# Gate columns of the modulation as running sums on VectorE, with weights loaded one k tile at a time

## The chip, the cores and the metric

The kernel runs on one core of a Trainium2 chip. The metric is the device time of one execution in microseconds (us), from several runs; less is better. Five engines work beside each other, each with a queue of its own that it works off in order: PE (TensorE: matmuls, and the loads of their weights as PEld), DVE (VectorE), ACT (ScalarE), POOL (GpSimd) and SP (SyncE, which here only issues transfers). Semaphores tie the queues together.

## The reference

One step of a network of one layer, on 128 context tokens and 256 latent tokens (384 in all), model width 4096. What matters here:

```python
mod = jax.nn.silu(c) @ w_ada + b_ada            # c_ctx for the context tokens
shift, scale, gate = jnp.split(mod, 3, axis=-1)  # 3 x 4096 columns
u = _rms_norm(h, norm_w) * (1.0 + scale) + shift
out, states = _mixer(u, ...)   # u @ w_in, 8 retention and 16 gated delta heads, both ways, @ w_out
h = h + gate * out
y = _rms_norm(h, final_norm_w)
```

`w_ada` is 4096 x 12288, `w_in` 4096 x 16448, `w_out` 4096 x 4096, all fp32. The modulation is wanted for two vectors only, that of the context and that of the latents. Shift and scale are needed before the input projection, the gate only after the output projection.

## The kernel before

**Projections.** A weight is used in k tiles of 128 rows (`NK` = 32 of them). A *piece* of a `Gemm` is one k tile of a group of 512 columns: its weights (128x512 fp32) land in a buffer `raw`, ScalarE rounds them into `wh` (L209), VectorE puts the rest into `wl` (L210), and PE multiplies both with the high and low part of the activations, `uh` and `ul`: 12 matmuls of 128x384 for a group of kind T (L258 to L260), 9 of 128x512 for kind N (L264 to L266). `wh` and `wl` are rings of `RING` = 5 tiles. Below, a weight tile is one such piece.

**Loads.** SP issues them in `load_piece` (L199): one call brings two k tiles, as two transfers of 256 KB, one for each run of 256 columns. The buffers `raw` are three; the gate pieces use them too.

**Stages.** Until about 770 us the shift and scale columns are computed (class `Ada`, tile `ada`) beside the first part of the input projection, whose partial sums are kept or spilled. Then the rest of the input projection follows, group after group: for each of eight p two groups of kind T and two of kind N. Beside it run the mixers: `gdn` (two gated delta heads, with a triangular solve on VectorE, L854 and L856) and `ret` (a retention head). The mixers are Python generators in `bg_list`. Each `yield` gives a time in ns, `slot(ns)` counts the matmul time that PE's queue has been given since, and when it is used up the next step is emitted (`bg_step`). `pace` stretches or shortens the steps, so that a head is done when its results are due; what is late at a due point is emitted at once (`bg_drain`). From about 2780 us the output projection runs, eight groups of 32 weight tiles. Its first group also fetches the mixers' results (`mix_load`, tile `mixl`, two buffers; `mix_put` splits them into `uh` and `ul`).

**Gate columns.** Class `Ada`, tile `adg`: for 512 columns 16 pieces. A piece loads four k tiles of 256 columns (512 KB) and issues four matmuls with the two vectors as the stationary side (`cst`, padded to 32 columns), each in another quarter of the array's columns (L322), so that the four row groups of the result hold four partial sums. `gate_done` copies them to SBUF on ScalarE, adds the four with a matmul by `sel` (L1184), adds the bias on VectorE and stores the rows in `d_gate`, from where the output projection fetches them, spread over the partitions. The 128 gate pieces are laid between the weight tiles of the N groups.

**Order.** `run_pieces` walks through the list of pieces. Loads and splits (`prepare`) are emitted ahead of the matmuls (`compute`), up to `room` pieces of a kind. So each engine's queue follows this list.

Of the kernel before, what the change touches and what calls it, by code (L numbers as in the profile page):

```python
# [7 lines left out]
F32 = mybir.dt.float32  # L8
F32R = mybir.dt.float32r
AF = mybir.ActivationFunctionType  # L10
ALU = mybir.AluOpType
# [4 lines left out]
D = 4096  # L16
NK = 32
T = 384
# [23 lines left out]
ADA_RING = 6  # L42
# [10 lines left out]
GATE = 1500  # L53
FMAX = 1.0
# [11 lines left out]
def hybrid_step(ctx: ExitStack, tc: tile.TileContext, x_prompt, x_sample, state_ret_fwd, state_ret_bwd,  # L66
# [35 lines left out]
    half_c = const.tile([128, 2, 12], F32, name="half_c")  # L102
    mid_ctx = ExitStack()
# [5 lines left out]
    cst = mid.tile([128, 2 * NK + 32], F32, name="cst")  # L109
    sel = mid.tile([128, 2], F32, name="sel")  # L110
# [81 lines left out]
    def load_piece(src, chunks, k0, nk, ring=None):  # L192
        shape = [128, nk, len(chunks), chunks[0][1]]
        if ring:
            raw = ring(shape)
        else:
            raw = wpool.tile(shape, F32, tag="raw", name="raw", bufs=3)
        for i, (c0, cn) in enumerate(chunks):
            SP.dma_start(out=raw[:, :, i, :],  # L199
                         in_=src[k0 * 128:(k0 + nk) * 128, c0:c0 + cn].rearrange("(k p) n -> p k n", p=128))  # L200
        return raw
# [11 lines left out]
    class Gemm:  # L213
# [6 lines left out]
        def __init__(self, kind, src, chunks, ks, done, pre=None, rows=None):  # L220
            self.kind, self.src, self.chunks, self.done, self.pre = kind, src, chunks, done, pre
            self.ks = ks
            self.rows = rows or (lambda k: k)
            self.ps = self.ps_alloc = self.raw = None
            self.batch, self.lend = 2, None
            self.hold = []
            self.pieces = [(self, i) for i in range(len(ks))]

        def prepare(self, i):
            if i % 2 == 0:  # L230
                self.raw = load_piece(self.src, self.chunks, self.rows(self.ks[i]), min(2, len(self.ks) - i))
            return split_tile(self.raw[:, i % 2], [128, 2, 256], self.lend and self.lend(i))

        def compute(self, i, hl):
# [16 lines left out]
            for n, ps in enumerate(self.ps):  # L251
                for m, (h, lo) in self.hold:
                    k = self.ks[m]
                    st, sp = m == 0, m == end
                    if self.kind == "T":
                        wh = h[:, n // 2, (n % 2) * 128:(n % 2) * 128 + 128]
                        wl = lo[:, n // 2, (n % 2) * 128:(n % 2) * 128 + 128]
                        PE.matmul(ps, wh, high(k), start=st, stop=False)  # L258
                        PE.matmul(ps, wh, low(k), start=False, stop=False)  # L259
                        PE.matmul(ps, wl, high(k), start=False, stop=sp)  # L260
                        slot(3 * 160)
                    else:
                        a, b = high(k)[:, n * 128:n * 128 + 128], low(k)[:, n * 128:n * 128 + 128]
                        PE.matmul(ps, a, h, start=st, stop=False)  # L264
                        PE.matmul(ps, a, lo, start=False, stop=False)  # L265
                        PE.matmul(ps, b, h, start=False, stop=sp)  # L266
                        slot(3 * 213)
                if i == end:
                    self.done(n, ps)
# [4 lines left out]
    class Gates:  # L274
# [9 lines left out]
        def prepare(self, i):  # L284
            raw = load_piece(w_in, [(16384, 64)], i, 8)
            return split_tile(raw[:, :, 0], [128, 8, 64])
# [14 lines left out]
    class Ada:  # L301
# [6 lines left out]
        def __init__(self, c0, width, ps_alloc, done, ring=None):  # L308
            self.c0, self.width, self.ps_alloc, self.done, self.ring = c0, width, ps_alloc, done, ring
            self.ps = None  # L310
            self.pieces = [(self, i) for i in range(0, width // 256 * NK, 4)]

        def prepare(self, i):
            return load_piece(w_ada, [(self.c0 + 256 * (i // NK), 256)], i % NK, 4, self.ring)

        def compute(self, i, raw):
            if self.ps is None:
                self.ps = self.ps_alloc()
            cs = slice(256 * (i // NK), 256 * (i // NK) + 256)
            for q in range(4):  # L320
                k = i % NK + q
                PE.matmul(self.ps[32 * q:32 * q + 32, cs], cst[:, 2 * k:2 * k + 32], raw[:, q, 0],  # L322
                          start=(k < 4), stop=(k >= NK - 4), tile_position=(0, 32 * q))
            slot(450)
            if i + 4 == self.width // 256 * NK:
                self.done(self.ps)
            return 1

# [18 lines left out]
    def run_pieces(pieces):  # L347
# [7 lines left out]
        out = {"do": 0, "ada": 0, "w": 0}  # L355
        room = {"do": len(pieces), "ada": ADA_RING - 1, "w": RING - 1}
        kind = lambda o: "do" if isinstance(o, Do) else ("ada" if isinstance(o, Ada) and o.ring else "w")
# [20 lines left out]
    V.tensor_copy(sel, con[:, C_SEL:C_SEL + 2])  # L378
# [795 lines left out]
    def gate_done(i):  # L1174
        def done(ps):
            sb = [mx.tile([128, T], F32, tag="gsb", name="gsb", bufs=2)[:, 0:256] for _ in range(2)]
            for j in range(2):
                A.copy(sb[j], ps[:, 256 * j:256 * j + 256])
            urgent.append(fin(ps, sb))

        def fin(ps, sb):
            yield GATE
            for j in range(2):
                PE.matmul(ps[0:2, 256 * j:256 * j + 256], sel, sb[j], start=True, stop=True)  # L1184
            yield
            c0 = 512 * i
            for j in range(2):
                G.dma_start(out=sb[j][0:2], in_=b_ada[0, 2 * D + c0 + 256 * j:2 * D + c0 + 256 * j + 256].partition_broadcast(2))
            yield 2000
            for j in range(2):  # L1190
                V.tensor_tensor(sb[j][0:2], ps[0:2, 256 * j:256 * j + 256], sb[j][0:2], op=ALU.add)
                G.dma_start(out=d_gate[:, c0 + 256 * j:c0 + 256 * j + 256], in_=sb[j][0:2])
        return done

# [19 lines left out]
    ada_q = []  # L1214
    for i in range(8):
        ada_q += Ada(2 * D + 512 * i, 512, lambda: ps_main.tile([128, 512], F32, tag="mm3", name="adg"), gate_done(i)).pieces
    for g, (kind, chunks) in enumerate(groups):
# [5 lines left out]
        if kind == "T":  # L1223
            pieces += gm.pieces
        else:
            n, rest = len(gm.pieces), 0
            if g % 2:
                rest = min(8, n // 2)
                cnt = len(ada_q) - 16 * (7 - g // 4)
            else:  # L1230
                cnt = min(16, max(0, 16 * n // (n + NK - reached.get(g + 1, 0) - 8)))
            pieces += gm.pieces[:LEAD] + interleave(gm.pieces[LEAD:n - rest], ada_q[:cnt]) + gm.pieces[n - rest:]
            ada_q = ada_q[cnt:]
    assert not ada_q
# [19 lines left out]
    def open_out():  # L1254
        bg_drain()
# [85 lines left out]
    run_pieces(pieces)  # L1341
# [52 lines left out]
```

## Time and profile before

| | |
|---|---|
| median of 3 runs | 3356.45 us (3355.21 to 3360.35) |
| the profiled execution | 3351.84 us, its span 3350.1 us |
| granted clock of TensorE | 0.991 |
| PE busy | 3254.2 us (97% of the span) |
| VectorE busy | 1845.3 us (55%) |
| ScalarE busy | 1201.5 us (36%) |
| moved by DMA | 626.14 MB, 187 GB/s on average |

PE's busy time counts matmuls from their start to a modelled end, so busy is not the same as at full speed. A row of a group has the line, engine, operation, what it writes and reads, how many, then the busy time and the mean duration of one in ns, and the idle time before them. The chain is the sequence of work, followed back from the last instruction, that set the end; it names at each moment one engine or transfer. In the rows of the transfers the last number is the median time from issue to landing.

### The profile page before, as it was taken

To read this page: it belongs to the slowest core of one execution; us is meant where nothing else is said; L and a number is where in the kernel's file an instruction comes from. 1 tells how busy PE (TensorE), PEld (TensorE's weight loads), DVE (VectorE), ACT (ScalarE), POOL (GpSimd) and SP (SyncE) were. 2 spreads that over 40 slices of the span, in tenths; PEclk is the share of its full clock that TensorE was granted. 3 is DMA by queue.
4 is the path that set the end of the run, shared out by engine and by line. 5 is a ranking of instruction groups with operands and counts; after the bars stand their busy time and mean duration, and the time that the engine had idled before them with its cause. 6 is when DMAs were issued, how large, how long until landed. Compare 5 with 4: busy or idle time off the path is not lost.

```text
span 3350.1 us, 51853 instructions
## 1 busy us (share of the span) xinstructions
PE 3254.2 (97%) x19312; PEld 2694.5 (80%) x19312; DVE 1845.3 (55%) x3811; ACT 1201.5 (36%) x2588; POOL 292.7 (9%) x463
## 2 busy tenths in 40 slices
PE   5999999999999999999999999999999999999998
PEld 2878888877799789689689689779779877788886
DVE  3664444337747646755756746746744855444444
ACT  3322222224244344244244244245244334333333
POOL 0000000001011011001011011011000002100000
PEclk7999999999999999999999999999999999999999
DMA  9989998965535545545644545554544555645445
GB/s 327 308 289 303 324 303 282 303 189 171 160 92 151 166 138 167 167 142 150 186 145 143 172 138 152 173 156 141 172 152 142 159 153 186 188 145 169 146 150 176
DMA packets 594237, 626.14 MB, mean 187 GB/s; under 512 B 38978, under 2 KB 577042, under 8 KB 593984
## 3 DMA queue, kind: packets, MB, share of 16 engines
q1 hardware_dynamic: 570096, 551.04, 52.0%
q0 software_dynamic: 23888, 71.79, 7.2%
q8 instruction: 151, 2.47, 0.3%
q14 instruction: 102, 0.84, 0.1%
HBM read 590.37 MB, written 32.33 MB: 186 GB/s over the span
## 4 chain that ended last, share of the span: by engine, by line
PE 81%; DVE 7%; DMA 6%; issue 3%; ACT 1%; SPq 1%; POOL 0%; ACTq 0%; POOLq 0%; DVEq 0%
PE mm L258 11%; PE mm L260 10%; PE mm L259 10%; PE mm L264 10%; PE mm L265 9%; PE mm L266 9%; PE ada L322 3%; DMA raw<-in_w_in_dram 3%; DVE tmp L854 3%; PE o L265 2%; PE o L266 2%; PE o L264 2%; DVE wl L210 2%; DMA mixl<-d_mix 2%; PE adg L322 1%
## 5 line engine op out<-in xcount | busy, mean ns | idle before, releaser
L210 DVE TENSOR_TENSOR wl<-raw,wh 128x512 fp32r<-128x512 f32 x1274 | 855.3, 686 | 947.4 <-ACT wh L209 931.6
L209 ACT CAST wh<-raw 128x512 fp32r<-128x512 f32 x1274 | 757.5, 620 | 1388.5 <-DMA raw<-in_w_in_dram 567.7
L264 PE MATMUL mm<-wh,uh 128*128 128x512 f32 x1920 | 782.4, 408 | 12.3 <-ACT rawt L564 5.9
L265 PE MATMUL mm<-wl,uh 128*128 128x512 f32 x1920 | 756.5, 394 | 18.0 <-DVE wl L210 17.4
L266 PE MATMUL mm<-wh,ul 128*128 128x512 f32 x1920 | 751.6, 391 | 0.0
L258 PE MATMUL mm<-uh,wh 128*128 128x384 f32 x2048 | 716.8, 350 | 4.1 <-DVE ul L555 2.7
L260 PE MATMUL mm<-uh,wl 128*128 128x384 f32 x2048 | 685.8, 335 | 0.0
L259 PE MATMUL mm<-ul,wh 128*128 128x384 f32 x2048 | 685.1, 335 | 0.0
L264 PEld LDWEIGHTS mm<-wh,uh 128*128 128x128 f32 x1920 | 361.3, 188 | 144.9 <-issue 44.2
L265 PEld LDWEIGHTS mm<-wl,uh 128*128 128x128 f32 x1920 | 361.7, 188 | 103.5 <-DVE wl L210 36.4
L258 PEld LDWEIGHTS mm<-uh,wh 128*128 128x128 f32 x2048 | 384.7, 188 | 48.7 <-issue 25.0
L266 PEld LDWEIGHTS mm<-wh,ul 128*128 128x128 f32 x1920 | 361.1, 188 | 76.7 <-DVE ul L1249 0.3
L259 PEld LDWEIGHTS mm<-ul,wh 128*128 128x128 f32 x2048 | 385.1, 188 | 3.9 <-issue 2.9
L260 PEld LDWEIGHTS mm<-uh,wl 128*128 128x128 f32 x2048 | 384.4, 188 | 0.0
L854 DVE TENSOR_TENSOR tmp<-M 48x4 f32<-48x4 f32 (+14 forms) x240 | 188.3, 784 | 3.4
L322 PE MATMUL ada<-adar,cst 128*32 128x256 f32 x2048 | 146.8, 403 | 23.4 <-DMA adar<-in_w_ada_dram 23.4
L645 DVE SCALAR_TENSOR_TENSOR acc<-rawt,cw,acc 128x126 f32<-128x126 f32 (+3 forms) x384 | 133.5, 410 | 11.9 <-ACT acc L640 11.9
L265 PE MATMUL o<-wl,uh 128*128 128x512 f32 x354 | 138.1, 390 | 0.9 <-DVE wl L210 0.9
L264 PE MATMUL o<-wh,uh 128*128 128x512 f32 x354 | 137.9, 389 | 1.0 <-ACT wh L209 1.0
L266 PE MATMUL o<-wh,ul 128*128 128x512 f32 x354 | 137.7, 389 | 0.0
L856 DVE TENSOR_REDUCE M<-tmp 48x2 f32<-48x4 f32 (+14 forms) x240 | 121.7, 507 | 8.4
L322 PEld LDWEIGHTS ada<-adar,cst 128*32 128x32 f32 x2048 | 53.8, 112 | 88.7 <-DMA adar<-in_w_ada_dram 42.9
(321 smaller groups left out, 2522.5 us busy)
## 6 DMA issues: line engine op xcount, KB each, us to landing
raw<-in_w_in_dram SPq DMA_DIRECT2D x1028, 256.0 KB, 3.7
adar<-in_w_ada_dram SPq DMA_DIRECT2D x256, 512.0 KB, 5.4
raw<-in_w_ada_dram SPq DMA_DIRECT2D x128, 512.0 KB, 3.7
raw<-in_w_out_dram SPq DMA_DIRECT2D x256, 256.0 KB, 3.1
rawt<-d_part POOLq DMA_DIRECT2D x26, 384.0 KB, 4.3
d_part<-spill POOLq DMA_DIRECT2D x9, 768.0 KB, 6.3
gr<-d_gc POOLq DMA_DIRECT2D x16, 384.0 KB, 7.3
d_mix<-mix POOLq DMA_DIRECT2D x32, 192.0 KB, 2.8
```

Of the source, the lines that this page charges most:

```text
L209: A.copy(h, raw)
L210: V.tensor_tensor(lo, raw, h.bitcast(F32), op=ALU.subtract)
L258: PE.matmul(ps, wh, high(k), start=st, stop=False)
L259: PE.matmul(ps, wh, low(k), start=False, stop=False)
L260: PE.matmul(ps, wl, high(k), start=False, stop=sp)
L264: PE.matmul(ps, a, h, start=st, stop=False)
L265: PE.matmul(ps, a, lo, start=False, stop=False)
L266: PE.matmul(ps, b, h, start=False, stop=sp)
L322: PE.matmul(self.ps[32 * q:32 * q + 32, cs], cst[:, 2 * k:2 * k + 32], raw[:, q, 0], start=(k < 4), stop=(k >= NK - 4), tile_position=(0, ...
L645: V.scalar_tensor_tensor(out=dst[:, lo:hi], in0=x[:, lo + o:hi + o], scalar=w(t), in1=dst[:, lo:hi], op0=ALU.mult, op1=ALU.add)
L854: V.tensor_tensor(t, M[0:48, 0:i, 0:i].rearrange("p j c -> p c j"), M[0:48, i:i + 1, 0:i].to_broadcast([48, i, i]), op=ALU.mult)
L856: V.tensor_reduce(M[0:48, i, 0:i], t, axis=AX.X, op=ALU.add)
```

## The change

- The gate columns are no longer matmuls. A new class `GateMod` loads one k tile of 512 columns (256 KB), and VectorE multiplies it, for each of the two vectors, with the vector's 128 values (one per partition) and adds it to a running sum `gacc` (128x512 for each). After 32 k tiles PE adds the 128 partitions of each sum with a matmul by a column of ones (tile `gsum`, 1x512 each), and VectorE adds the bias.
- The 256 gate pieces are laid evenly between all weight tiles from the second part of the input projection on, the output projection included, up to 96 weight tiles before the end (`with_gates`). The last k tile of a block waits for an N group or the output projection.
- Each gate piece adds 1000 ns to the time that the mixers' next step waits for (`GATE_NS`). It counts no matmul time.
- Weights of the projections come one k tile at a time: one transfer of 256 KB with both runs of columns (`load_pair`). The buffers `raw` are four, each half as large, and the gate pieces share them; up to two gate pieces are prepared ahead.
- `cst` and `ones` live to the end. The urgent steps are emptied before the output projection's buffers open.

```diff
-            raw = wpool.tile(shape, F32, tag="raw", name="raw", bufs=3)
-        for i, (c0, cn) in enumerate(chunks):
-            SP.dma_start(out=raw[:, :, i, :],
-                         in_=src[k0 * 128:(k0 + nk) * 128, c0:c0 + cn].rearrange("(k p) n -> p k n", p=128))
+    def load_pair(src, ca, cb, k):
+        raw = wpool.tile([128, 2, 256], F32, tag="raw", name="raw", bufs=4)
+        a = src[k * 128:(k + 1) * 128, ca:ca + 256]
+        SP.dma_start(out=raw, in_=bass.AP(a.tensor, a.offset, [a.ap[0], (cb - ca, 2), a.ap[1]]))
+        return raw
...
+    class GateMod:
+        slots = 0.0
...
+        def prepare(self, k):
+            return load_piece(w_ada, 2 * D + self.c0, 512, k, 1)
+
+        def compute(self, k, raw):
+            if k == 0:
+                self.acc = wpool.tile([128, 2, 512], F32, tag="gacc", name="gacc", bufs=1)
+            for b in range(2):
+                a, cb = self.acc[:, b], cst[:, 2 * k + b:2 * k + b + 1]
+                if k == 0:
+                    V.tensor_scalar(a, raw[:, 0], scalar1=cb, scalar2=None, op0=ALU.mult)
+                else:
+                    V.scalar_tensor_tensor(out=a, in0=raw[:, 0], scalar=cb, in1=a, op0=ALU.mult, op1=ALU.add)
+            clock["next"] += GATE_NS
+            if k == NK - 1:
+                urgent.append(self.finish())
+            return 1
+
+        def finish(self):
+            yield GATE
...
+            for b in range(2):
+                PE.matmul(ps[row[b]], ones, acc[:, b], start=True, stop=True, tile_position=(0, 32 * b))
...
-        room = {"do": len(pieces), "ada": ADA_RING - 1, "w": RING - 1}
+        room = {"do": len(pieces), "ada": ADA_RING - 1, "w": RING - 1, "gate": 2}
...
-    def gate_done(i):
-        def done(ps):
-            sb = [mx.tile([128, T], F32, tag="gsb", name="gsb", bufs=2)[:, 0:256] for _ in range(2)]
-            for j in range(2):
-                A.copy(sb[j], ps[:, 256 * j:256 * j + 256])
...
-    for i in range(8):
-        ada_q += Ada(2 * D + 512 * i, 512, lambda: ps_main.tile([128, 512], F32, tag="mm3", name="adg"), gate_done(i)).pieces
...
-            pieces += gm.pieces[:LEAD] + interleave(gm.pieces[LEAD:n - rest], ada_q[:cnt]) + gm.pieces[n - rest:]
...
+    def with_gates(pieces, first):
+        n = [isinstance(o, Gemm) for o, _ in pieces[first:]].count(True) - GATE_LAG
+        units = [p for c0 in range(0, D, 512) for p in [None] * 4 + GateMod(c0).pieces]
...
+            credit += len(units) / max(1, n)
...
+                if u and u[1] == NK - 1 and not (obj.src is w_out or obj.kind == "N" and 2 <= i < len(obj.pieces) - 8):
+                    break
```

How the order of the engines moves shows at three places: in PE's queue in the N groups, where the gate rows leave; in the queues of SP and VectorE, where a gate piece is loaded among the weight tiles and summed behind later ones; and in PE's queue at the end of the last retention head. They stand with the steps of the prediction that rest on them. The first of them, in SP's queue, once more at another stretch of the input projection's second part, before:

```order
L199 DMA raw_17393<-in_w_in_dram 128x2x256 x2
L199 DMA raw_17427<-in_w_in_dram 128x2x256 x2
L199 DMA raw_17440<-in_w_ada_dram 128x4x256
L199 DMA raw_17476<-in_w_in_dram 128x2x256 x2
L199 DMA raw_17504<-in_w_ada_dram 128x4x256
```

and after, at a like place:

```order
L205 DMA raw_12030<-in_w_in_dram 128x2x256
L205 DMA raw_12053<-in_w_in_dram 128x2x256
L198 DMA raw_12059<-in_w_ada_dram 128x512
L205 DMA raw_12077<-in_w_in_dram 128x2x256
L205 DMA raw_12101<-in_w_in_dram 128x2x256
L205 DMA raw_12129<-in_w_in_dram 128x2x256
```

A row with x2 is one buffer of two k tiles, brought by two transfers; a gate piece was four k tiles of 256 columns and is now one of 512.

More of the change, by code (lines that the diff above doesn't have):

```diff
@@ L102, in hybrid_step @@
     half_c = const.tile([128, 2, 12], F32, name="half_c")
+    cst = const.tile([128, 2 * NK + 32], F32, name="cst")
+    ones = const.tile([128, 1], F32, name="ones")
     mid_ctx = ExitStack()
@@ L327, in compute, with __init__ @@
             return 1
+    class GateMod:
+        slots = 0.0
+        def __init__(self, c0):
+            self.c0 = c0
+            self.pieces = [(self, k) for k in range(NK)]
+        def prepare(self, k):
[15 more added lines that the diff above has]
+            yield GATE
+            acc, cs = self.acc, slice(2 * D + self.c0, 2 * D + self.c0 + 512)
+            ps = ps_main.tile([128, 512], F32, tag="mm3", name="gsum")
+            row = [slice(32 * b, 32 * b + 1) for b in range(2)]
+            for b in range(2):
+                PE.matmul(ps[row[b]], ones, acc[:, b], start=True, stop=True, tile_position=(0, 32 * b))
+            yield
+            for b in range(2):
+                G.dma_start(out=acc[row[b], 1 - b], in_=b_ada[0:1, cs])
+            yield 2000
+            for b in range(2):
+                V.tensor_tensor(acc[row[b], b], ps[row[b]], acc[row[b], 1 - b], op=ALU.add)
+                G.dma_start(out=d_gate[b:b + 1, self.c0:self.c0 + 512], in_=acc[row[b], b])
     class Do:
@@ L354, in run_pieces @@
         ready, nxt = {}, 0
-        out = {"do": 0, "ada": 0, "w": 0}
-        room = {"do": len(pieces), "ada": ADA_RING - 1, "w": RING - 1}
-        kind = lambda o: "do" if isinstance(o, Do) else ("ada" if isinstance(o, Ada) and o.ring else "w")
+        out = {"do": 0, "ada": 0, "w": 0, "gate": 0}
+        room = {"do": len(pieces), "ada": ADA_RING - 1, "w": RING - 1, "gate": 2}
+        kinds = {Do: "do", Ada: "ada", GateMod: "gate"}
+        kind = lambda o: kinds.get(type(o), "w")
         for idx, (obj, i) in enumerate(pieces):
@@ L377, in hybrid_step @@
     V.tensor_copy(neg.rearrange("p d s -> p (d s)"), con[:, C_NF:C_NF + 256])
-    V.tensor_copy(sel, con[:, C_SEL:C_SEL + 2])
+    G.memset(ones, 1.0)
     def psb():
@@ L1222, in hybrid_step @@
             dues[id(gm), max(0, len(gm.pieces) - PRE)] = ("gdn", g // 4 - 1)
[L1223 to L1231, printed above, removed]
-            pieces += gm.pieces[:LEAD] + interleave(gm.pieces[LEAD:n - rest], ada_q[:cnt]) + gm.pieces[n - rest:]
-            ada_q = ada_q[cnt:]
-    assert not ada_q
+        pieces += gm.pieces
     rowk = [(2 * (j // 4) if j % 4 >= 2 else 16 + 2 * (j // 4)) + j % 2 for j in range(NK)]
@@ L1340, in hybrid_step @@
             pieces += gm.pieces
-    run_pieces(pieces)
+    def with_gates(pieces, first):
+        n = [isinstance(o, Gemm) for o, _ in pieces[first:]].count(True) - GATE_LAG
+        units = [p for c0 in range(0, D, 512) for p in [None] * 4 + GateMod(c0).pieces]
+        out, credit = pieces[:first], 0.0
+        for obj, i in pieces[first:]:
+            out.append((obj, i))
+            if not isinstance(obj, Gemm):
+                continue
+            credit += len(units) / max(1, n)
+            n -= 1
+            while credit >= 1 and units:
+                u = units[0]
+                if u and u[1] == NK - 1 and not (obj.src is w_out or obj.kind == "N" and 2 <= i < len(obj.pieces) - 8):
+                    break
+                credit -= 1
+                units.pop(0)
+                if u:
+                    out.append(u)
+            credit = min(credit, 2.0)
+        assert not units
+        return out
+    run_pieces(with_gates(pieces, first))
     bg_drain()
```

55 lines of the change are left out of this document (21 added, 34 removed).

## The prediction

> **What bounds the kernel now.** I read the totals and the summed chain first, then the stages, then the chain of the stage in which the gate pieces lie.
>
> ```profile
> span 3350.1 us, 51853 instructions
> PE 3254.2 (97%) x19312; PEld 2694.5 (80%) x19312; DVE 1845.3 (55%) x3811; ACT 1201.5 (36%) x2588; POOL 292.7 (9%) x463
> ...
> PE 81%; DVE 7%; DMA 6%; issue 3%; ACT 1%; SPq 1%; POOL 0%; ACTq 0%; POOLq 0%; DVEq 0%
> ```
>
> ```profile
> 770.00:2780.00 2010.00, 1976.57 (x11660) 1652.04 (x11659) 1241.94 (x2685) 782.20 (x1788) 227.76 (x340) 1.00 0.51 154
> ...
> 2890.00:3170.00 280.00, 280.00 (x1236) 231.51 (x1235) 119.74 (x179) 93.86 (x169) 14.37 (x25) 1.00 0.52 160
> ```
>
> A stage row gives its length, the busy time of PE, PEld, DVE, ACT and POOL, the clock, the DMA share and GB/s. PE is busy 98% of the time from 770 to 2780 us (second part of the input projection, beside the mixers) and 100% in the output projection, at full clock. VectorE is free for 768 of 2010 us in the first and 160 of 280 in the second. Yet PE is not the whole chain of the first:
>
> ```profile
> by line: PE mm L264 11.9%; PE mm L265 11.0%; PE mm L266 10.9%; PE mm L258 10.5%; PE mm L260 10.4%; PE mm L259 10.4%; DVE tmp L854 5.0%; DMA raw<-in_w_in_dram 4.2%; DVE wl L210 3.4%; issue 2.6%; PE adg L322 2.3%; DVE M L856 1.9%; PE bg L1121
> ```
>
> This is the chain between 800 and 2780 us. The triangular solve on VectorE (L854, L856) with the weight splits caught in it (L210) holds 10.3%, 204 us; waiting for weight tiles to land 4.2%, 83 us. The gate matmuls that go (adg) are 2.3% of 1980 us, 45.5 us.
>
> **Gate matmuls leave PE.** PE's order in an N group before: one gate piece between two weight tiles.
>
> ```order
> L266 MATMUL mm_15101<-wh,ul_4419 128x512
> L322 MATMUL adg<-raw,cst 32x256 x4
> L264 MATMUL mm_15099<-wh,uh_4477 128x512
> L265 MATMUL mm_15099<-wl,uh_4477 128x512
> L266 MATMUL mm_15099<-wh,ul_4478 128x512
> ```
>
> All 128 such rows are gone afterwards (each is eight matmul records), and eight pairs of column sums of 1x512 take the place of sixteen sums of 2x256.
>
> ```profile
> 1612.96 0.40 PE L264 MATMUL mm<-wh,uh 128*128 128x512 f32 x1
> 1613.19 0.39 PE L265 MATMUL mm<-wl,uh 128*128 128x512 f32 x1
> 1613.42 0.39 PE L266 MATMUL mm<-wh,ul 128*128 128x512 f32 x1
> 1613.74 0.64 PE L322 MATMUL adg<-raw,cst 128*32 128x256 f32 x8
> 1614.31 0.50 PE L264 MATMUL mm<-wh,uh 128*128 128x512 f32 x1
> 1614.65 0.40 PE L265 MATMUL mm<-wl,uh 128*128 128x512 f32 x1
> ```
>
> ```profile
> L322 PE MATMUL adg<-raw,cst 128*32 128x256 f32 x1024 | 81.8, 391 | 2.1 <-DMA raw<-in_w_ada_dram 2.1
> L1121 PE MATMUL bg<-Sr,qkT 128*128 128x512 f32 x64 | 30.0, 591 | 0.0
> L1184 PE MATMUL adg<-gsb,sel 128*2 128x256 f32 x32 | 8.2, 378 | 0.0
> ```
>
> ```profile
> 1408.73 0.57 PE adg L322 x8
> ```
>
> Projection matmuls start 0.23 us apart. From L266 at 1613.42 to L265 at 1614.65 two steps should take 0.46 and take 1.23, so a piece costs PE 0.77 us, and 128 cost 99 us. That is the most that can be won here. On the chain a piece is 0.57 us (the last row is one of them), so 45.5 us are 80 of the 128 pieces; the others run while PE has slack under the solve. I take 80 x 0.77 = 62 us; the ends are 45.5 and 99. The column sums: out go 8.2 us of PE, in come 32 records of 512 columns, at L1121's 30.0 us for 64 some 15, or half that if the two column positions overlap: -1 to +7 us, taken as 0. The ScalarE copies and bias additions of a block were short and off the chain.
>
> **Running sums on VectorE.** 256 weight pieces of 128x512 with two operations each, 512 in all.
>
> ```profile
> L645 DVE SCALAR_TENSOR_TENSOR acc<-rawt,cw,acc 128x255 f32<-128x255 f32 x96 | 45.8, 477 | 0.0
> L645 DVE SCALAR_TENSOR_TENSOR acc<-rawt,cw,acc 128x126 f32<-128x126 f32 x96 | 33.0, 344 | 11.9 <-ACT acc L640 11.9
> ...
> L1308 DVE TENSOR_TENSOR hw<-to,wo 128x512 f32<-128x512 f32 x24 | 16.5, 689 | 0.6
> ```
>
> The same operation grows by 1.03 ns per element, which gives 742 ns at 512; the plain addition of that shape has 689. I take 0.69 us, since two in a row overlap a little: 1.38 us a piece, 353 us in all. It fits in the idle time of both stages (928 us), so it is hidden where PE binds. It is not hidden in the solve: 204 us of chain at 2.6 us a tile (below) hold 78 tiles, and with one gate piece per 3.6 tiles (256 over about 920: the 1019 weight tiles from 800 us on, without the last 96) 22 pieces, 30 us. The planner now charges 1.0 us of pace for each piece, so the solve spreads over more tiles instead; I take +8, with ends 0 and +30.
>
> **Loads one k tile at a time, and the four buffers.** Before, three buffers of two k tiles each; now four of one, shared with the gate pieces. SP's order in the input projection before and after, then VectorE's after (raw_11894, 11988 and 12059 are gate pieces, other raws weight tiles):
>
> ```order
> L199 DMA raw_17251<-in_w_in_dram 128x2x256 x2
> L199 DMA raw_17300<-in_w_in_dram 128x2x256 x2
> L199 DMA raw_17312<-in_w_ada_dram 128x4x256
> L199 DMA raw_17349<-in_w_in_dram 128x2x256 x2
> L199 DMA raw_17382<-in_w_ada_dram 128x4x256
> ```
>
> SP after, another stretch of the same kind:
>
> ```order
> L198 DMA raw_11894<-in_w_ada_dram 128x512
> L205 DMA raw_11945<-in_w_in_dram 128x2x256
> L205 DMA raw_11951<-in_w_in_dram 128x2x256
> L205 DMA raw_11982<-in_w_in_dram 128x2x256
> L198 DMA raw_11988<-in_w_ada_dram 128x512
> L205 DMA raw_12008<-in_w_in_dram 128x2x256
> ```
>
> VectorE after, at that place:
>
> ```order
> L215 TENSOR_TENSOR wl_11985<-raw_11982,wh_11984 128x512
> L1117 TENSOR_TENSOR Wr_11979<-Wr_11979 128x384
> L1120 TENSOR_TENSOR Wr_11979<-Wr_11979,ident_71 128x128
> L1128 TENSOR_TENSOR rt_12002<-rawt_10997,rcon_84 128x256
> L1129 TENSOR_TENSOR rt_12002<-rawt_10997,rcon_84 128x256
> L215 TENSOR_TENSOR wl_12011<-raw_12008,wh_12010 128x512
> L355 SCALAR_TENSOR_TENSOR gacc_10793<-raw_11894,cst_73,gacc_10793 128x512 x2
> ```
>
> Gate piece 11894 is loaded ahead of weight tiles 11945 to 12008 and summed behind their splits; by then 11988, the next one, holds a buffer too. So the gates hold one or two of the four buffers and weight tiles run on two or three: the load of a tile waits for the split of the tile two or three before it. That makes a loop, load, ScalarE cast, VectorE subtraction, next load. Two rounds of this kind stand in the chain already, one for weights (which before loads two tiles a round), one for the mixer results, which have two buffers:
>
> ```profile
> 1377.21 0.37 SPq L199
> 1377.63 3.15 DMA raw<-in_w_in_dram
> 1380.87 0.63 ACT wh L209
> 1381.52 0.69 DVE wl L210
> ...
> 2825.75 2.82 DMA mixl<-d_mix
> 2828.60 0.52 ACT uh L1248
> 2829.14 0.57 DVE ul L1249
> 2830.00 2.86 DMA mixl<-d_mix
> ```
>
> ```profile
> raw<-in_w_in_dram SPq DMA_DIRECT2D x1028, 256.0 KB, 3.7
> ...
> raw<-in_w_out_dram SPq DMA_DIRECT2D x256, 256.0 KB, 3.1
> ```
>
> A round of weights took 5.00 us (1377.21 to 1382.21), of which 0.42 is the issue of the second half, now gone; from 3.1 us to landing, 0.63, 0.69 and 0.1 between them it is 4.5. A gate piece stands in front of one split in 3.6, 0.38 us on average: 4.9. With 2.2 buffers on average that is 2.22 us a tile. What PE needs:
>
> ```profile
> L210 DVE TENSOR_TENSOR wl<-raw,wh x755: 637/684/695, 801.7 to 2777.8; 128x512 fp32r<-128x512 f32 x189
> ...
> L210 DVE TENSOR_TENSOR wl<-raw,wh x36: 680/692/695, 1519.9 to 1599.0; 128x512 fp32r<-128x512 f32 x36
> ...
> L210 DVE TENSOR_TENSOR wl<-raw,wh x198: 679/692/694, 2900.6 to 3298.8; 128x512 fp32r<-128x512 f32 x198
> ```
>
> 755 tiles in 1980 us, 2.62 each; in light stretches 36 in 80, 2.22; in the output projection 198 in 400, 2.02 (2.04 without the last block's edge). So the loop is no loss in the light part of the first stage (which I put at half, 380 tiles), and costs 0.18 us on the 130 tiles of the output projection that still carry gates (256 less the last 96 and the first 30, which wait for the mixers anyway): +23 us. Ends: 0 (three buffers) and, with exactly two (2.45 us), 130 x 0.41 + 380 x 0.23 = +140.
>
> [...] The rows of this case say 3.1 to 3.7 for SyncE's loads, so the sum goes by them.
>
> **Mixers later.** The planner's charge for gates and the missing gate slots delay the mixers. Before, PE's order for the last retention head has projection rows between its steps:
>
> ```order
> L1121 MATMUL bg<-Sr,qkT 128x512 x2
> L264 MATMUL mm_26000<-wh,uh_483 128x512
> L265 MATMUL mm_26000<-wl,uh_483 128x512
> L266 MATMUL mm_26000<-wh,ul_484 128x512
> L264 MATMUL mm_26001<-wh,uh_483 128x512
> ```
>
> Afterwards its second half is emitted in one piece, drained at the point where the first output block needs it:
>
> ```order
> L1169 MATMUL bg<-Sr,qkT 128x512 x2
> L1177 MATMUL bg<-rawt,Wr 128x256
> L1178 MATMUL bg<-rawt,Wr 128x256
> L1179 MATMUL bg<-rawt,Wr 128x256
> L1180 MATMUL bg<-rawt,Wr 128x256
> L1181 MATMUL bg<-rawt,Wr 128x256
> L1203 MATMUL bg<-rawt,kd 128x256 x4
> L1214 MATMUL bg<-ident,o_r 128x128 x6
> ```
>
> ```profile
> 2780.00:2890.00 110.00, 104.20 (x458) 83.55 (x458) 59.09 (x109) 47.85 (x97) 24.62 (x44) 1.00 0.60 183
> ```
>
> Nothing hides the handovers between PE, ScalarE and VectorE there, and two rounds of about 4.3 us for the mixer results (the rows above) follow, with the weights already in the rings as the only cover. PE was idle for 6 us of this stretch before; I take +8, from 0 to +20. Edits left (ones, constants moved, single loads while the shift and scale columns run): 0, from -8 to +8.
>
> **Sum.** -62 + 0 + 8 + 23 + 8 = -23 us. The profiled execution took 3351.84 us, its span 3350.1, the median of the three runs is 3356.45, 4.6 us above it. 3351.8 - 23 = 3329, and 3333 us against the median: faster by 0.7%.
>
> **Rivals.** All of PE's gain: the rings stay full, and the slack under the solve shrinks with the charge; 99 us less, 8 back for the mixers: 3265 us. For it speaks VectorE's idle half; against it that only 80 pieces are on the chain. The load loop binds: if weight tiles get two buffers nearly always, every tile above 2.264 us ((62 - 16) = 130 x (t - 2.04) + 380 x (t - 2.22)) turns the gain into a loss; at 2.36, halfway to 2.45, it is +95 - 46 = +49, 3405 us. For it speaks the pattern in SP's and VectorE's orders, against it that buffers come free a tile sooner at times. [...] VectorE binds: all 30 us in the solve, and 20 from the drain: 3333 + 22 + 12 = 3367. No change: gains and losses cancel, 3356.
>
> **Chances.** Forecast 0.45 (own range 3300 to 3350), full gain 0.14, loop 0.26, VectorE 0.07, no change 0.08. A measurement here tells 0.2%, 7 us, from nothing. Of the forecast's 0.45 nearly all is faster: 0.57 with the full gain; same 0.11; slower 0.32. The range 3265 to 3412 leaves out the far side of both rivals.
>
> **What would show it.** Right: adg gone from PE, PE's busy share about as before in a span 20 to 30 us shorter, the output projection's first 130 tiles near 2.2 us with ScalarE waiting for raw, gacc at 1.38 us a pair, DVE busy near 2190 us. Wrong: tiles at 2.04 there (full gain), or SP's queue waiting for wl and gacc throughout and PE idle in even gaps in light stretches (loop), or a longer stay of the chain on L854's successors (VectorE).

## The result, and the profile after

The changed kernel takes 3546.35 us (median of 4 runs, 3541.41 to 3551.83) against 3356.44 us for the kernel before on the same chip: 1.0564 times as long, 95% interval 1.0544 to 1.0584. The forecast was 3333 us, with 3265 to 3412 as its range. The kernel became slower by 190 us instead of faster by 23, and the time lies 134 us beyond the slow end of the range.

The head of the page of the changed kernel, its granted clock, and the two stages that were shown of before:

```profile
span 3549.7 us, 51176 instructions
PE 3277.9 (92%) x18288; PEld 2728.2 (77%) x18288; DVE 2180.3 (61%) x4322; ACT 1220.5 (34%) x2572; POOL 292.1 (8%) x464
```

```profile
core 0: 3549.7 us, clock 0.967
```

```profile
770.00:2780.00 2010.00, 1848.51 (x10001) 1588.91 (x10000) 1407.30 (x2901) 752.34 (x1679) 208.83 (x309) 0.97 0.49 140
2890.00:3170.00 280.00, 252.55 (x1180) 196.15 (x1179) 160.77 (x295) 103.40 (x211) 36.52 (x63) 0.97 0.55 167
```

PE lost 1024 records and yet is busy 24 us longer. In the first stage it is idle for 161 of 2010 us (33 before) and its clock is 0.97 (1.00 before). The clock's records are 1.00 or 0.50, so 0.967 means that 2 x 0.033 x 3549.7 = 234 us passed at half clock; before, at 0.991, it was 60 us. Such a share had no fixed price here: one run of the kernel before had a clock of 0.938 and took 3367.34 us, only 10 us over the median on its chip. VectorE is busy 2180 us, the forecast was 2190: the size of the sums was right, also row by row.

```profile
L355 DVE SCALAR_TENSOR_TENSOR gacc<-raw,cst,gacc 128x512 f32<-128x512 f32 x496 | 348.8, 744 | 0.0
...
L367 PE MATMUL gsum<-gacc,ones 128*1 128x512 f32 x32 | 13.2, 698 | 11.2 <-DVE gacc L355 11.2
```

What ends the waits of ScalarE's casts (the changed kernel, then the kernel before; us in total, times, longest), and how long a load takes in the changed kernel:

```profile
ACT wh L214 <- DMA raw<-in_w_in_dram: 935.3, 420, 10.5
```

```profile
ACT wh L209 <- DMA raw<-in_w_in_dram: 567.7, 174, 8.5
```

```profile
raw<-in_w_in_dram SPq DMA_DIRECT2D x1028, 256.0 KB, 2.9
raw<-in_w_ada_dram SPq DMA_DIRECT2D x256, 256.0 KB, 2.9
raw<-in_w_out_dram SPq DMA_DIRECT2D x256, 256.0 KB, 2.9
```

A load is faster than forecast (2.9 us, not 3.1), but the casts wait 935 us for loads of the input projection instead of 568. So the loads start late. The output projection shows the loop whole: the splits of the part with gates, and the chain from 3060 to 3350 us.

```profile
L215 DVE TENSOR_TENSOR wl<-raw,wh x126: 678/692/695, 3040.3 to 3339.2; 128x512 fp32r<-128x512 f32 x126
```

```profile
by line: DMA raw<-in_w_out_dram 44.9%; ACT wh L214 10.6%; DVE wl L215 10.4%; issue 6.6%; PE o L271 5.5%; PE o L270 5.3%; PE o L272 5.3%; DVE gacc L355 4.9%; PE gsum L367 1.5%; DVE hw L1324 1.1%; ACT to L1325 0.8%; DVE to L1320 0.8%; DVE to 
```

126 tiles in 298.9 us are 2.37 us each, where PE needs 2.04. Load, cast and subtraction are 66% of the chain, PE's three matmuls 16%; before, PE was 100% busy here. Some rows of SP's and VectorE's queues in that stretch show why:

```profile
3186.94 0.33 SPq L198 DMA_DIRECT2D raw<-in_w_ada_dram  x1
3187.54 6.04 SPq L205 DMA_DIRECT2D raw<-in_w_out_dram  x3
3194.58 0.33 SPq L198 DMA_DIRECT2D raw<-in_w_ada_dram  x1
...
3204.34 0.33 SPq L198 DMA_DIRECT2D raw<-in_w_ada_dram  x1
```

```profile
3193.14 1.41 DVE L355 SCALAR_TENSOR_TENSOR gacc<-raw,cst,gacc 128x512 f32<-128x512 f32 x2
...
3202.90 1.41 DVE L355 SCALAR_TENSOR_TENSOR gacc<-raw,cst,gacc 128x512 f32<-128x512 f32 x2
```

Two gate tiles are under way most of the time. The tile asked for at 3186.94 is the one summed at 3202.90, and some 30 ns after the end of a sum SP gives its buffer to the next but one gate tile (3194.58, 3204.34). Counted over all 37 gate loads from 3040 to 3340 us, a gate tile keeps its buffer for 14.5 us from issue to the end of its sum, 1.79 buffers on average; over the 216 loads from 800 to 3030 us 17.3 us and 1.68 buffers. The transfer is 2.9 us of that.

Where the time went, by weight tiles: the time in us between the first matmuls of two tiles on PE, counted in each trace (a tile has 12 records of 384 columns or 9 of 512). Tiles 280 to 1030 are the part beside the mixers, 1030 to 1060 hold the mixers' end, 1060 to 1210 the output projection with gates.

| kernel | 280-1030 | 1030-1060 | 1060-1210 |
|---|---|---|---|
| before | 1976.7 | 66.6 | 307.0 |
| changed | 2085.5 | 103.6 | 358.2 |
| before, no gate pieces | 1866.7 | 65.5 | 307.0 |
| changed, no gate pieces | 1866.9 | 65.6 | 307.4 |
| sums alone | 1940.2 | 98.3 | 309.6 |
| loads alone | 2022.5 | 100.1 | 351.2 |
| loads alone, own buffers | 1897.1 | 103.9 | 309.3 |
| the same, loads from GpSimd | 1866.6 | 100.4 | 306.7 |
| the same, no charge | 1893.9 | 72.5 | 308.8 |
| changed, six buffers | 1976.1 | 111.0 | 313.1 |

### The profile page after: what moved, and what is told of

The parts are those of the page before. It is cut to its first block, busy times and chain, and to the rows that moved or that the text cites. A ratio compares the mean times of both kernels' runs of the same rounds, so it can differ in the third digit from the quotient of the medians.

```text
span 3549.7 us, 51176 instructions
## 1 busy us (share of the span) xinstructions
PE 3277.9 (92%) x18288; PEld 2728.2 (77%) x18288; DVE 2180.3 (61%) x4322; ACT 1220.5 (34%) x2572; POOL 292.1 (8%) x464
## 5 line engine op out<-in xcount | busy, mean ns | idle before, releaser
L215 DVE TENSOR_TENSOR wl<-raw,wh 128x512 fp32r<-128x512 f32 x1274 | 861.9, 687 | 903.4 <-ACT wh L214 883.7
L214 ACT CAST wh<-raw 128x512 fp32r<-128x512 f32 x1274 | 778.2, 620 | 1698.4 <-DMA raw<-in_w_in_dram 935.3
L271 PE MATMUL mm<-wl,uh 128*128 128x512 f32 x1920 | 775.8, 404 | 50.4 <-DVE wl L215 49.6
L272 PE MATMUL mm<-wh,ul 128*128 128x512 f32 x1920 | 763.6, 398 | 0.0
L264 PE MATMUL mm<-uh,wh 128*128 128x384 f32 x2048 | 733.6, 358 | 26.8 <-ACT wh L214 15.0
L266 PE MATMUL mm<-uh,wl 128*128 128x384 f32 x2048 | 697.7, 341 | 2.2 <-DVE wl L215 1.5
L265 PE MATMUL mm<-ul,wh 128*128 128x384 f32 x2048 | 695.6, 340 | 0.0
L271 PEld LDWEIGHTS mm<-wl,uh 128*128 128x128 f32 x1920 | 370.1, 193 | 162.4 <-DVE wl L215 91.9
L270 PEld LDWEIGHTS mm<-wh,uh 128*128 128x128 f32 x1920 | 369.7, 193 | 162.4 <-ACT wh L214 32.0
L272 PEld LDWEIGHTS mm<-wh,ul 128*128 128x128 f32 x1920 | 369.4, 192 | 76.1
L355 DVE SCALAR_TENSOR_TENSOR gacc<-raw,cst,gacc 128x512 f32<-128x512 f32 x496 | 348.8, 744 | 0.0
```

Source lines behind the costliest of these rows:

```text
L214: A.copy(h, raw)
L215: V.tensor_tensor(lo, raw, h.bitcast(F32), op=ALU.subtract)
L355: V.scalar_tensor_tensor(out=a, in0=raw[:, 0], scalar=cb, in1=a, op0=ALU.mult, op1=ALU.add)
```

## The experiments

Times are medians; ratios are against runs of the kernel before on the same chip, whose medians were 3353.4 to 3356.9 us. Theory S says that gate tiles hold the weights' buffers, theory V that the sums stand in the way on VectorE. The handover is the stretch of tiles 1030 to 1060, where the last mixers end and the output projection starts.

**The parts one by one.** Without gate pieces (`run_pieces(pieces)`; the gate is only its bias):

> The changed kernel without gate pieces: no loads of gate columns, no sums; the gate is the bias alone (written once at the start). All theories expect TensorE's whole saving here, since nothing of the gates is left: 3356 less about 99 us, 3250 to 3275 us. If the loads of one k tile with four buffers were at fault by themselves, it would stay above 3340 us.

Measured 3242.64 us, ratio 0.9662 (0.9634 to 0.9690). With sums but no gate loads (the operation multiplies and adds the running sum itself, `in0=a` in place of `in0=raw`):

> Only the sums on VectorE: 512 operations of 128x512 at the places where they stand, on the running sum itself, without loads of gate columns (so the gate is wrong in its product, and no buffer is held). Theory S (the gate pieces hold weight buffers): fast, 3260 to 3320 us. Theory V (the sums stand in front of the splits in VectorE's queue): 3480 us or more.

3350.16 us, 0.9977 (0.9962 to 0.9991): the sums alone cost 107.5 us, between what the two theories expected and as much as all gate matmuls had been thought to. By the table 73 us of it lie beside the mixers, 33 in the handover and 2 in the output projection. With loads but sums of 8 of 512 columns (`raw[:, 0, 0:8]`):

> Only the loads: gate pieces are loaded and keep their buffers as in the changed kernel, but the sums take 8 of 512 columns. Theory S: still slow, 3480 to 3550 us, ScalarE waiting for raw some 1000 us. Theory V: 3300 us or less.

3479.56 us, 1.0368 (1.0328 to 1.0409): 237 us for loads that nobody computes on. And the whole change with each sum emitted as soon as two more weight tiles are loaded and split:

> The changed kernel with the sum of a gate piece emitted as soon as two more weight tiles have been loaded and split, instead of behind the fourth or fifth: all work is done, a gate piece keeps its buffer for about two weight loads. Theory S: weight tiles have three buffers most of the time, 3300 to 3420 us. Theory V: nothing changes on VectorE's load, 3500 us or more.

3447.0 us, 1.0271 (1.0227 to 1.0315): 99 us back, again between the two ranges. Counted over the loads from 800 to 3030 us, a gate tile now keeps its buffer for 12.3 us instead of 17.3, so the gates hold 1.23 buffers instead of 1.68. The sums also stand at other places of VectorE's queue here, which this run does not separate. Both theories hold, S with the larger share. PE and its waits for splits, without gate pieces, then with sums alone:

```profile
PE 3149.1 (97%) x18256; PEld 2686.6 (83%) x18256; DVE 1839.0 (57%) x3794; ACT 1213.2 (37%) x2572; POOL 279.2 (9%) x434
...
PE mm L271 <- DVE wl L215: 19.1, 24, 2.5
```

```profile
PE 3193.9 (95%) x18288; PEld 2706.1 (81%) x18288; DVE 2172.2 (65%) x4322; ACT 1212.5 (36%) x2572; POOL 292.3 (9%) x464
...
PE mm L271 <- DVE wl L215: 38.2, 37, 2.5
PE mm L270 <- ACT rawt L612: 20.5, 9, 5.6
```

Of the 107 us, 62 are idle time of PE (span less busy, 91.3 against 153.7) and 45 a longer busy time, some 13 of them the new column sums; the rest goes with a clock of 0.981 instead of 0.995, without a run that shows it by itself. No engine became the bound: VectorE has 65%. Small delays of 2 to 6 us added up.

What the gate pieces had cost in the kernel before, with its paired loads (`pieces += gm.pieces`, no gate pieces):

> The kernel before, with its loads of two k tiles, without gate pieces (the gate is only its bias). The forecast held at most 99 us for the gate pieces, 0.77 us each, but the changed kernel without gate pieces is 114 us faster than before. If loading one k tile at a time brought the rest: 3256 us or somewhat more here. If the gate pieces cost more than the forecast said (buffers, DMA): 3243 us, and single loads bring nothing.

3230.07 us, 0.9622 (0.9608 to 0.9637). So the pieces cost 126 us, and loading one k tile at a time, with four buffers of 256 KB for three of 512 and the small edits beside it, loses 12.6 us rather than bringing any. All of it lies ahead of tile 250, beside the shift and scale columns (774.1 us for 761.9); from there on the two run alike, as the table shows.

**The charge and the handover.** `GATE_NS = 0.0` in the whole change:

> The whole change, but the planner charges nothing for a gate piece (GATE_NS 0 instead of 1000), so the mixers are spread as if the sums were free. Theory M: the handover to the output projection lost 33 us (30 tiles from the 1030th: 66.6 us before, 103.6 after) because the charge and the missing slots put the mixers off; without the charge most of that comes back, 3510 to 3520 us. Theories S and V (weight buffers held by gate pieces, sums in front of splits): the same work comes a little earlier and the tiles keep their pace, 3535 to 3560 us.

3551.02 us, 1.0577 (1.0556 to 1.0598). Tiles 1030 to 1060 do fall from 103.6 to 79.1 us, but tiles 280 to 1030 rise by 21. The same for sums alone, and (below) for loads with own buffers:

> Sums alone (3350.16 us, 107 above the run without gate pieces; its tiles 1030 to 1060 took 98.3 us), without the planner's charge. If 33 of the 107 us are the mixers drained at the end (theory M2): 3315 to 3322 us. If the sums then hold up the solve and the splits as much as they are allowed to (theory V, as the whole change without the charge did): 3340 to 3355 us.

3360.55 us, 1.0013 (1.0000 to 1.0027): 71.5 us there, but 38.5 more ahead of it. Theory M2, by which the charge puts the mixers off and so costs the time at the handover, falls: the charge moves the loss from one place to the other. That the handover had grown by 37 us did not make it the cause.

**Whose buffers, whose queue.** Loads alone again, with two gate buffers of their own and four for weights (`tag="graw", bufs=2`, paid for by a running sum of 8 columns):

> The run with gate loads and sums of 8 columns again (3479.56 us, 237 above the run without gate pieces), but the gate pieces have two buffers of their own and the weight tiles keep all four (the space is there because the running sum is only 8 columns wide). Theory S, held buffers: most of the 237 us is gone, 3250 to 3290 us. Rival O, the order in SP's queue: a gate load still waits there for the sum two gates earlier, which stands behind the newest split in VectorE's queue, and holds up the weight loads behind it; then it stays above 3400 us. Rival B, DMA traffic: the 32 MiB of gate columns cost the same from any buffer, 3480 us.

3310.11 us, 0.9859 (0.9833 to 0.9886). 170 of the 237 us were the shared buffers (up to 8 of them the shorter column sums: PE was busy 9.7 us with them in the run before, 1.6 us here). The result lies between the ranges of S and O. The gate columns are 256 loads of 256 KB, 64 MiB and not the 32 of rival B, which falls all the same. What SP then waits for first:

```profile
SPq L198 <- DVE gacc L353: 811.7, 190, 16.8
SPq L205 <- DVE wl L215: 755.9, 431, 12.4
```

Gate loads wait 812 us in SP's queue for sums, and the weight loads behind them wait along. The same kernel with gate loads from GpSimd's queue (`G.dma_start` for `SP.dma_start`), then also without the charge:

> The run with gate loads, sums of 8 columns and two gate buffers of their own (3310.11 us, 67 above the run without gate pieces), with the gate loads issued from GpSimd's queue instead of SP's. Theory O: the rest is the order in SP's queue, where a gate load that waits for the sum two gates earlier (SP waited 811.7 us in 190 such waits) holds up the weight loads behind it; then 3245 to 3275 us. Rival B, DMA traffic: the additional 32 MiB make weight tiles land later from any queue, 3300 to 3315 us. Rival P: the waits move to GpSimd's queue and hold up the mixers' transfers there, slower than 3310 us.

> Gate loads from GpSimd's queue into two buffers of their own, sums of 8 columns (3276.55 us, 34 above the run without gate pieces), now without the planner's charge for a gate piece. In that run only tiles 1030 to 1060 are slower than without gate pieces in total (100.4 us against 65.6). Theory M2: these 35 us are mixers put off by the charge and drained ahead of the output projection; without it 3243 to 3252 us, and gate loads as such cost nothing. Rival: the drain has another cause (the gates' own steps, GpSimd's queue), 3265 to 3285 us.

3276.55 us, 0.9764 (0.9745 to 0.9784), and 3284.26 us, 0.9782 (0.9753 to 0.9810). 33.6 us came back with the other queue, as theory O had it; the waits stand on GpSimd now (`POOL graw L198 <- DVE gacc L353: 826.8, 130, 30.8`) and hold up less. From tile 280 to 1030 and in the output projection the first of them is as fast as without gate loads (1866.6 and 306.7 us). The 34 us that remain are in the mixers, with the charge at their end, without it ahead. What makes them longer (GpSimd's busier queue, the blocks' own steps) stays open. So does one rival of theory O: loads from GpSimd also go through another DMA queue (q0 of the page moves 138.89 MB instead of 71.76), and no run tells this from the order in SP's queue. The loads themselves were not shorter there, 3.5 us against 3.2 from SP.

**Both repairs in the whole change.** Six buffers for weight and gate tiles, one split tile less in the ring (`RING = 4`, `bufs=6`):

> The whole change with six buffers of 256 KB for weight and gate tiles instead of four, paid for with one split tile less in the ring between VectorE and PE (4 instead of 5). Theory S, too few buffers: gate pieces hold two of six, four are left for weights as in the run without gate pieces, and most of the 237 us that gate loads cost comes back: 3380 to 3420 us. Rival V and the shorter ring: PE waits for splits as before or more, 3500 us or above.

3406.11 us, 1.0157 (1.0137 to 1.0178): 140 us back, as theory S had it. Then gate loads from GpSimd as well, and no charge:

> The whole change with both repairs and without the charge: six buffers shared by weights and gates (ring of split tiles 4), gate loads from GpSimd's queue. With six buffers alone it took 3406.11 us. If theories S, O and V describe all of it, what is left is the 107 us of the sums and some 10 to 30 us of the shorter ring and of gates still holding two of six buffers: 3350 to 3385 us, no better than before. Rival: GpSimd's queue, where mixers' transfers now stand behind gate loads that wait for a weight tile's buffer, costs more than SP's: above 3406 us.

3429.36 us, 1.0214 (1.0184 to 1.0244). The causes do not just add up, and the rival named above came true; how the 23 us over six buffers alone divide between the two edits was not run. Here gate tiles still share the weights' buffers, so GpSimd's queue waits for splits, with the mixers' transfers behind:

```profile
POOL raw L198 <- DVE wl L215: 768.1, 124, 12.8
```

**Single loads with the gates on PE.** Weights one k tile at a time in six buffers of 256 KB, gate matmuls on PE in 256 pieces of two k tiles:

> The loading part of the change alone: weights one k tile at a time, in six buffers of 256 KB (the space of the three pair buffers), and the gate matmuls stay on PE, in pieces of two k tiles so that a piece fits such a buffer. If single loads are harmless or better where there are buffers enough: 3335 to 3356 us. If they cost by themselves (twice as many gate pieces, more descriptors in SP's queue): 3365 us or more.

3414.4 us, 1.0173 (1.0156 to 1.0189), slower, but the loads do not show as the reason: the output projection took 307.0 us as before. The gate matmuls, as many as before (81.8 us there), are dearer in twice as many pieces (the row below, and 2029.6 us for 1976.7 from tile 280 to 1030). The traces show why. Before, the four matmuls of a piece, each in its own quarter of the array's columns, start 7 ns apart, with records of 0.39 us, and the piece lasts 0.64 us (81.8 us busy in 128 pieces); here a piece of two is busy 0.61 us (157.1 us in 256), nearly as long as one of four.

```profile
L327 PE MATMUL adg<-raw,cst 128*32 128x256 f32 x1024 | 157.1, 391 | 0.0
```

So this run does not tell what single loads cost; the pair without gate pieces does.

**What a short wait does to the clock.** The kernel before without gate pieces, with sixteen waits in the output projection (a small matmul, a ScalarE copy, n GpSimd copies, a small matmul that reads the last):

> The kernel before without gate pieces (3230.07 us, PE at full clock through the output projection), with sixteen waits put into PE's queue in the output projection, one every 12 weight tiles: a small matmul, a ScalarE copy of its result, a chain of 0, 1, 2, 4, 6, 9, 12 or 16 GpSimd copies of 128x128 (each length twice), and a small matmul that reads the end. It shows what an idle PE of a known length does to the granted clock. Theory C: waits of 1 to 3 us are enough for a stretch of half clock after them, as in the trace of the changed kernel, so each costs its own length and some 1.7 us (half of a stretch of 3.4 us) more; all sixteen then cost some 27 us beyond the idle time. [...]

One profiled execution, 3303.8 us of span against 3228.2. Two waits, and the stretches behind the waits of 1.64 us (2826), 2.89 us (2880), 5.03 us (2941) and 6.46 us (2973):

```profile
2828.00 0.38 PE L347 MATMUL gap<-gapt,ident 128*128 128x128 f32 x1 [1.64 <-POOL gapt L346]
...
2979.98 0.58 PE L347 MATMUL gap<-gapt,ident 128*128 128x128 f32 x1 [6.46 <-POOL gapt L346]
```

```profile
2828.00:2841.00 13.00, 13.00 (x58) 10.82 (x59) 7.09 (x12) 4.99 (x13) 0.00 (x0) 1.00 0.37 121
2884.00:2894.00 10.00, 10.00 (x46) 8.27 (x45) 2.77 (x4) 2.50 (x4) 2.54 (x5) 1.00 0.80 234
2946.60:2950.00 3.40, 3.24 (x9) 2.66 (x10) 0.00 (x0) 0.00 (x0) 2.95 (x6) 0.50 0.38 78
2980.00:2990.00 10.00, 10.00 (x37) 8.19 (x38) 1.98 (x3) 1.29 (x3) 0.00 (x0) 0.79 0.17 54
```

The eight waits up to 2.18 us left the clock alone. Of the two of 2.89 us the second was followed by half clock (the row below). All six of 5.03 us and more had it too; in five of them it began before the wait was over, 3.7 to 5.2 us after its start. Seven stretches of 3.41 or 6.83 us make 37.6 us, and PE worked in 31 of them.

```profile
3116.50:3120.00 3.50, 3.50 (x11) 2.75 (x11) 0.00 (x0) 0.41 (x1) 2.50 (x5) 0.61 0.61 92
```

Theory C is too strong below 2.2 us, where no wait of this run was followed by half clock; at 2.89 us one of two was. In the changed kernel half clock follows a wait of 2.21 us:

```profile
1624.37 0.44 PE L264 MATMUL mm<-uh,wh 128*128 128x384 f32 x1 [2.21 <-ACT wh L214]
```

```profile
1624.70:1628.10 3.40, 3.40 (x11) 3.00 (x10) 2.24 (x6) 1.58 (x4) 0.00 (x0) 0.50 0.41 107
```

In the changed kernel's records after 770 us, half clock follows (it begins in the gap or up to 3.5 us behind it) 1 of 98 gaps of 0.15 to 1 us, 5 of 39 of 1 to 2 us, 16 of 23 of 2 to 3 us and 15 of 17 longer ones. Before, there were only three gaps of 2 us or more, two of them followed by it.

**A version that beats both.** Gate columns 0 to 2047 stay matmuls on PE. Columns 2048 to 4095 become running sums in the output projection, where SBUF is free, with three buffers of their own; weights load in pairs as before:

```diff
+            raw = oc["sb"].tile([128, 512], F32, tag="graw", name="graw", bufs=3)
+            SP.dma_start(out=raw, in_=w_ada[k * 128:(k + 1) * 128, c:c + 512])
...
-    for i in range(8):
+    for i in range(4):
         ada_q += Ada(2 * D + 512 * i, 512, ...)
```

> Attempt at a faster kernel: the kernel before with its paired loads; gate columns 0 to 2047 stay matmuls on PE, columns 2048 to 4095 become running sums on VectorE, but in the output projection, where SBUF is free, with three buffers of their own (128 pieces beside 208 tiles of 2.04 us). PE saves half of what all gate pieces cost (126 us): 63, so 3293 us if sums and loads are hidden. VectorE has per tile 0.69 for the split, 0.85 for sums and some 0.2 for the ends of the blocks, 1.74 of 2.04 us. Rival V: sums in front of splits make PE wait all the same, as in the run with sums alone (+107 us for 512 sums): 54 of the 63 us lost, 3347 us.

> As the run with four gate blocks on VectorE in the output projection, but with five: 160 pieces beside 208 tiles. If the sums stay hidden PE saves 79 of 126 us: 3277 us. VectorE then has 1.95 of 2.04 us per tile; rival V: the edge is crossed, PE waits for splits in most blocks, and it is slower than the run with four, 3300 to 3340 us.

3413.07 us, 1.0182 (1.0167 to 1.0197), and with five blocks 3466.77 us, 1.0341 (1.0324 to 1.0358). Slower than even theory V had said, though V seemed to explain it. SP's waits from 2900 to 3350 us of the first say otherwise:

```profile
SPq L341 <- DVE gacc L355: 292.3, 103, 8.1
```

So only the queue of the gate loads was changed (`G.dma_start`):

> The attempt with four gate blocks on VectorE in the output projection (3413.07 us; its output projection took 78 us per 30 tiles instead of 61.2, and SP waited 292 us there at gate loads for sums), with the gate loads issued from GpSimd's queue. Theory O: weight loads are no longer held up and the sums are hidden, 3290 to 3300 us, faster than both kernels. Rival V: sums in front of splits in VectorE's queue make PE wait, 3340 us or more.

> The same with five gate blocks in the output projection (3466.77 us with SP's queue). Theory O: 3275 to 3290 us if VectorE, with 1.95 of 2.04 us a tile, keeps up. Rival V: it does not, and it is slower than the run with four, 3310 to 3380 us.

3305.21 us, 0.9850 (0.9835 to 0.9864), and 3301.05 us, 0.9841 (0.9825 to 0.9858), a little above theory O's ranges: 108 and 166 us by one word, 1.5% faster than before and 7% faster than the change. In the first, from 2800 to 3250 us, the waits are as long, on a queue where nothing urgent stands behind:

```profile
POOL graw L341 <- DVE gacc L355: 298.1, 109, 7.7
```

With four blocks PE needs 311.9 us for tiles 1060 to 1210 (307.0 before) beside the same sums (388.4 with SP's queue). Theory V falls for this stage; with five blocks it is 321.3. No run here tests what the other queue does for bandwidth, but it decided what waits behind a load that itself waits, and moving the loads was worth 108 us.

## Why the prediction was wrong

| step | forecast, us | measured, us | from |
|---|---|---|---|
| gate matmuls leave PE | -62 (-99 to -45.5) | -126 | before without gate pieces |
| single-tile loads, smaller buffers (in the other edits) | 0 (-8 to +8) | +12.6 | the two kernels without gate pieces |
| running sums | +8 (0 to +30) | +107.5 | sums alone |
| gate loads, loop, buffers | +23 (0 to +140) | +237 | loads alone |
| mixers later | +8 (0 to +20) | none seen by itself | three runs without the charge |
| sum | -23 | +231; whole change +190 | the parts overlap by 41 |

- **PE's gain** was mis-sized, beyond its end. 0.77 us a piece gives 99, the sums of the four row groups 8 more; I took 80 of 128 pieces because the chain showed 80, and held the others to be free. The rest, 126 - 107 = 19 us, is not separated. The buffers that gate pieces held are a candidate: SP waited for them before as well.

```profile
SPq L199 <- PE adg L322: 197.4, 76, 6.6
```

- **Column sums** were right: 13.2 us for 8.2, +5, within -1 to +7. But PE stood 11.2 us in front of them, waiting for the last running sum (the row of L367 above), and no term held that.
- **Running sums**: the duration was right (a pair 1.41 us for 1.38), the step "hidden where PE binds" failed. PE at 98% of a stage with mixers does not mean that work on VectorE is free there: PE's waits for splits doubled (19.1 to 38.2 us) and others came, since splits and mixer steps stand in VectorE's queue with the sums; which of them pays most was not separated. In the output projection, where the mixers' steps are gone, the sums are nearly free (sums alone 309.6 us for 307.4 there).
- **The loop** was the right mechanism, told as a rival with 0.26, and the number of buffers was right too: 4 - 1.79 = 2.2 for weights. What failed is the round of 4.9 us. In the output projection it was 2.37 x 2.2 = 5.2 us, so a tile took about the 2.36 of that rival. The trace says the same: from issue to the end of its split a weight tile keeps its buffer for 5.24 us there (128 loads) and for 6.50 us beside the mixers (714 loads from 800 to 2780 us). Beside the mixers cast and split wait 2.0 us of that, in the output projection 0.6, and 2.2 or 2.3 buffers don't cover it; I had taken one undisturbed round for the whole stage and put no loss there. It was the larger part: 2022.5 for 1866.9 us from tile 280 to 1030 by loads alone. That SP's queue passes on a gate load's wait to the weight loads was nowhere in the sum: moving the gate loads to GpSimd's queue brought 34 us with own buffers and 108 in the version above.
- **Mixers later**: the handover grew by 37 us, more than the end of 20, yet without the charge the total stayed. It was a place, not a cause.
- **Missing altogether**: the clock. Every term counted a wait at its own length. After 770 us, 180 us passed at half clock, 20 before, and PE was busy in 152 and 7 of them. Projection matmuls of 128x512 started 0.43 us apart there, 0.23 at full clock (medians in the changed kernel's trace), so by an estimate (half of the difference) up to 72 us of PE's busy time are the clock. The busy row is longer too, 3277.9 us against 3149.1 without gate pieces, of which the new sums are 13.2; part of it is the modelled end of the last matmul in front of a gap, whose record is 0.40 us on average at the 177 gaps over 0.15 us after 770 us (53 gaps before), where matmuls in an unbroken row start 0.17 or 0.23 us apart. No run takes the lower clock apart from the waits ahead of it. In the changed kernel's trace it followed 15 of 17 gaps over 3 us, and 16 of 23 of 2 to 3 us already.
- Of the signs named, "SP's queue waiting for wl and gacc throughout" came true, but it tells little. SP waited for wl in the kernel before too (`SPq L199 <- DVE wl L210: 1256.4, 416, 11.1`), and most of all in the changed kernel without gate pieces (`SPq L205 <- DVE wl L215: 1671.1, 877, 12.8`). The casts' waits for loads of the input projection tell the loop better: 446.4 us without gate pieces, 935.3 in the changed kernel. SP's rows in the changed kernel:

```profile
SPq L205 <- DVE wl L215: 1384.9, 838, 12.4
...
SPq L198 <- DVE wl L215: 121.9, 73, 9.0
SPq L198 <- DVE gacc L355: 117.7, 134, 0.9
```

## What to carry to other kernels

A tile that is loaded early and used late is charged by the time that it keeps a buffer from a faster stream (17.3 us here, 2.9 of them its transfer); give it buffers of its own (170 of 237 us came back), and a DMA queue in which nothing urgent stands behind its wait (108 us). Work moved to an idle engine was hidden only in the stage where that engine was in nobody's chain (the sums alone cost 73 us beside the mixers and 2 in the output projection), so put it in such a stage, and do not count a share of idle time over a stage with handovers. For a wait of PE of 2 us or more, count the lower clock too: here half clock followed 31 of 40 such gaps in the changed kernel, nearly always for 3.41 or 6.83 us (once 10.24), which cost an estimated half of the stretch at most.

## What was not expected of the hardware

- In the changed kernel PE went to half clock after 16 of 23 gaps of 2 to 3 us, for 3.41 us or more, longer than the gap itself. In the run with sixteen waits PE worked 31 us at half clock, so an estimated 15 of the 76 us that the run lost are the clock (half of the 31); 49.7 us are the waits themselves.
- A gate piece of two matmuls was busy nearly as long as one of four (0.61 and 0.64 us), so the same number in twice as many pieces was busy 157.1 us for 81.8.
- With own gate buffers a 256 KB load from GpSimd's queue took 3.5 us to land, one of the input projection from SP's queue 3.2 in the same run; the queue with the slower transfer gave the faster kernel (3276.55 us; 3310.11 with the gate loads on SP's queue).
